# Idle TensorE matmuls around a Strassen-like feed-forward: two of 512 columns in place of eight groups

## The chip, the cores and the metric

The kernel runs on one core of a Trainium2 chip, in one launch. The metric is the device time of an execution in microseconds (us), the median of several runs. A profiled execution is one more execution, taken with the hardware profiler; its own time and its span (first to last instruction) are given beside the median. TensorE does matmuls, VectorE (DVE) and ScalarE (ACT) do elementwise work, GpSimd (POOL) and SyncE (SP) mostly issue DMAs.

## The reference

One encoder layer on 512 tokens of 1024 features, in float32, cut to its outline:

```python
n = rms_norm(h, mix_norm_g); proj = n @ w_in            # 1024 -> 512 + 4 * 1024
ya = s5_branch(...)                                     # state-space scan, both directions, + GLU
yb = sgu_branch(...)                                    # gated mixing within chunks of 128 tokens
h = h + (gate_a * (ya @ w_proj_a) + gate_b * (yb @ w_proj_b)) @ w_out
h = h + memory_cross_attention(rms_norm(h), memn, w_q, w_k, w_v, w_xo)
h = h + (silu(hn @ w_gate) * (hn @ w_up)) @ w_down      # hn = rms_norm(h); d_ff = 2816
return rms_norm(h, final_norm_g)
```

The change lies in the last product but one: the gate and up parts of the feed-forward.

## The kernel before

Every float32 operand of a large product is split into a part `hi` rounded to the type fp32r (ACT copies, line 85) and a rest `lo` (DVE subtracts, line 86), and each product is three matmuls on TensorE, hi x hi, hi x lo and lo x hi, summed in one PSUM bank (`mm3`, lines 347 to 352, and `product`, 1267 to 1278). The weights come from HBM in blocks of 512 KB. A plan written out by hand lists all blocks in the order of use; `next_w` (322 to 333) hands out the next one, issues loads some entries ahead and splits two entries ahead. `tick` (445) runs work that was put off by `later`. The recording layer then orders each engine's instructions by a simulated timeline, except those that `in_order` pins to the program's order.

In the stage before, attention's output product adds to the residual rows `h`. As each block of 128 rows is complete, it is normalised and turned by TensorE (`to_feat`, line 509: tiles `ptr`, four transposes each), and ACT and DVE write it as `fn`, features by tokens, split into `fn_hi` and `fn_lo` (lines 511 and 512), and whole as `full` (513). The last rows' turnings fall between the first matmuls of the feed-forward.

Gate and up have 2816 columns each. The last 256 columns are computed directly: `gate_part` (1458) for the gate, in two halves of the tokens, T0 and T1, and `feat` (1474) for up; these are the `pf` matmuls of line 350. The other 2560 columns are ten jobs (`UNITS`, line 313), gate and up in turn, 512 columns each. A job is a product of 2 x 2 blocks (token halves by feature halves K0 and K1, and by column halves) with seven block products in place of eight. Their operands are kept in `ops`: products 1, 2, 4 and 7 read parts of `fn`, products 5, 6 and 3 read sums of parts, kept in tiles `s`. Each of the seven is one call of `product`, 24 matmuls of 256 columns on banks `px`, `pv` or `pq`; "a block" below is such a call. The loop over the jobs (1531 to 1575) runs the products in the order 5, 6, the next job's 1, 7, the next job's 2, 4, 3. Product 1 of the first job (`unit_start`, 1465) and its product 2 (`unit_second`, 1467) stand between the gate's parts. In the first job K0's half for T1 is overwritten by a difference (line 1542), which product 7 reads from then on.

Between the blocks of the second and the third job (i = 1 and 2) the kernel runs idle work on TensorE: `between` (1522 to 1529) takes an idle bank and issues, by a string, transposes of the identity (`t`) or a matmul of 512 columns on `fn` (`p`), pinned in order. Nothing reads the results. The strings are "tt", then "p" or "pt", then "t" or "ttt", then "tttt" or "tt": eight groups, 15 transposes and 2 matmuls.

Behind the jobs the down product (lines 1634 to 1672) uses seven block products too, in matmuls of 512 columns on banks `dx`, `dv` and `dq` (line 350); two of its chunks are already run within the last job.

Idle tiles, the turnings and the up part's banks come in turn from one pool of three PSUM banks (`aux`, line 80).

Of the kernel before, what the change touches and what calls it, by code (L numbers as in the profile page):

```python
# [17 lines left out]
P = 128  # L18
# [34 lines left out]
def hybrid_layer_kernel(  # L53
# [8 lines left out]
    nc = tc.nc  # L62
# [14 lines left out]
    def bank(name):  # L77
        return pm.tile([P, 512], F32, tag="mm", name=name)

    def aux(name, shape=(P, 512)):  # L80
        return pa.tile(list(shape), F32, tag="aux", name=name)

    def split(dst_hi, dst_lo, src):

        hi = nc.scalar.copy(dst_hi, src)  # L85
        lo = nc.vector.tensor_tensor(dst_lo, src, dst_hi.bitcast(F32), ALU.subtract)  # L86
        if pinned[0]:
            in_order(hi)
            in_order(lo)
# [3 lines left out]
    in_order = tc.keep_in_program_order  # L93
# [228 lines left out]
    def next_w(*key):  # L322
        i = used_w[0]
        used_w[0] += 1
        assert len(plan[i][0]) == len(key) and plan[i][0][1:] == key[1:] and plan[i][0][0] is key[0]
        for j in range(i, min(i + FAR + 1, len(plan))):
            begin(j, i)
            if j - 1 >= len(tiles) and j - 1 <= i + SPLITS:
                split_w(j - 1)
        for j in range(len(tiles), min(i + SPLITS + 1, len(plan))):  # L330
            split_w(j)
        tile_, tiles[i] = tiles[i], None
        return tile_
# [45 lines left out]
    def feat_block(ps, x, act, nk, kpt, tsl, fresh=True):  # L379

        kb, hi, lo = x
        for j in range(2):
            cs = slice(j * P, (j + 1) * P)
            for k in range(kpt):
                kk = kb + k
                mm3(ps[j][:, tsl], (hi[:, k, cs], lo[:, k, cs]), (act[0][:, kk, tsl], act[1][:, kk, tsl]),
                    kk == 0 and fresh, kk == nk - 1, not fresh)
# [57 lines left out]
    def tick(us=5.2):  # L445

        side["now"] += us / 5.2
        run_due()
        side["credit"] = min(side["credit"] + us * side["rate"], us)
        while side["credit"] > 0.0 and side["gen"] is not None:  # L450
            try:
                used = next(side["gen"])
            except StopIteration:
                side["gen"] = None
                return
            if used is None:
                side["credit"] = 0.0
                return
            side["credit"] -= used
# [6 lines left out]
    ident = cp.tile([P, P], F32, name="ident")  # L466
# [58 lines left out]
    def token_slot(name, off=(0, 0)):  # L525

        return halves_at(sp.tile([P, 2 * KD * T + 128], F32R, tag="B", name=name), KD, T, off)
# [6 lines left out]
    idle = aux("idle", (P, P))  # L534
# [732 lines left out]
    def product(ps, u, q, start, ops):  # L1267

        hi, lo = next_w(u[0], u[1], q)
        for j in range(2):  # L1270
            cs = slice(j * P, (j + 1) * P)
            for k in range(4):
                a = (hi[:, k, cs], lo[:, k, cs])
                b = (ops[q][0][:, k, :], ops[q][1][:, k, :])
                for i, (x, y) in enumerate(((0, 0), (0, 1), (1, 0))):
                    nc.tensor.matmul(ps[:, j, :], a[x], b[y], start=start and j == k == i == 0,  # L1276
                                     stop=k == 3 and i == 2, skip_group_check=True)
        tick(2.7)

    def unit_bank(name):  # L1280
        return bank(name).rearrange("p (j t) -> p j t", j=2)
# [79 lines left out]
    fn_hi, fn_lo = token_slot("fn", APART)  # L1361
# [37 lines left out]
    def acts(unit, f):  # L1399

        if unit < 4:
            return (a_up, a_lo_)[f][:, 2 * unit:2 * unit + 2, :]
        if not rest:
            rest.append(fp.tile([P, KD, T], F32, tag="full", name="rest", bufs=1))
        return rest[0][:, 2 * f:2 * f + 2, :]
# [23 lines left out]
    def sum4():  # L1429
        V.tensor_tensor(a12, a12, a11, ALU.add)  # L1430
        make_op(3, 4, a12)

    fn_q = lambda ks, ts: (fn_hi[:, ks, ts], fn_lo[:, ks, ts])
    ops = {1: fn_q(K0, T0), 2: fn_q(K1, T0), 7: fn_q(K0, T1), 4: fn_q(K1, T1)}

    def unit_start(u):
        x, v = unit_bank("px"), unit_bank("pv")
        product(x, u, 1, True, ops)
        nc.scalar.copy(v, x)
        return x, v  # L1440

    def put(u, f, ts, src):
        dst = acts(u[1] // 512, f)[:, :, ts]
        if u[0] is w_gate:
            nc.scalar.activation(dst, src, AF.Silu)
        else:
            nc.vector.tensor_tensor(dst, dst, src, ALU.mult)

    def unit_second(u, v):
        product(v, u, 2, False, ops)  # L1450
        put(u, 0, T0, v)
# [6 lines left out]
    def gate_part(i, ts):  # L1458
        if ts is T0:
            ws.append((4 * i,) + next_w(w_gate, 4 * i, 4, FS, 256))  # L1460
        feat_block(ps, ws[i], fn, KD, 4, ts, ts is T0)
        tick(2.7)

    gate_part(0, T0)
    begun = unit_start(UNITS[0])
    gate_part(1, T0)
    unit_second(UNITS[0], begun[1])
    for i in range(2):
        gate_part(i, T1)
    for j in range(2):  # L1470
# [15 lines left out]
    def make_tokens(q, c):  # L1486

        if c % 2 or (q, c // 2) in made or (q, c) == (1, 0) and not last_job:
            return
        c //= 2  # L1490
        hi, lo = made[q, c] = sums_place((1, 2, 4)[len(made) % 3], 4, 256)
        f, ts = {1: (0, T0), 5: (0, T1), 6: (0, T1), 2: (1, T0), 7: (0, T0), 3: (1, T0), 4: (1, T1)}[q]
        for src, ks in token_pieces(f, ts, c):
            split(hi[:, ks], lo[:, ks], src)
        a, b_, c_, d_ = (token_pieces(f_, ts_, c) for ts_ in (T0, T1) for f_ in (0, 1))
        for (q11, _), (q12, _), (s21, _), (q22, _) in zip(a, b_, c_, d_):
            if q == 5:
                V.tensor_tensor(s21, s21, q11, ALU.subtract)
            elif q == 3:
                V.scalar_tensor_tensor(q11, s21, -1.0, q22, ALU.mult, ALU.subtract)  # L1500
            elif q == 2:
                V.tensor_tensor(q12, q12, s21, ALU.add)
# [14 lines left out]
    def down_product(ps, q, start, chunks=range(CHUNKS)):  # L1517
        for c in chunks:
            rows_product(ps, q, c, next_w(w_down, q, c), (0, 1), slice(0, 512), start and c == 0, c == CHUNKS - 1,
                         chunks[0] == c > 0)  # L1520

    def between(*what):

        rest_ = aux("idle")
        for w in what:
            if w == "t":
                in_order(nc.tensor.transpose(rest_[:, 0:P], ident, ident))
            else:
                in_order(nc.tensor.matmul(rest_, ops[1][0][:, 0, 0:P], fn_hi[:, 0, :], start=True, stop=True))

    for i, u in enumerate(UNITS):
        final = i == len(UNITS) - 1
        x, v = begun
        q = unit_bank("pq")
        if i in (1, 2):
            between(*"tt")
        product(q, u, 5, True, ops)
        if final:
            last_job.append(u)
            make_tokens(1, 0)  # L1540
        if i == 0:
            split(*fn_q(K0, T1), s3)
        if i in (1, 2):
            between(*"pt"[:i])
        product(x, u, 6, False, ops)
        u2 = stp[0].tile([P, 2, 256], F32, tag="u2", name="u2", bufs=2)
        u3 = np_.tile([P, 2, 256], F32, tag="ev", name="u3", bufs=2)
        nc.scalar.copy(u2, x)
        if not final:
            begun = unit_start(UNITS[i + 1])  # L1550
        else:
            dx = [bank(f"dx{t}") for t in range(2)]
            down_product(dx, 1, True, range(1))
        if i in (1, 2):
            between(*"tttt"[:i * 2 - 1])
        product(x, u, 7, False, ops)
        nc.scalar.copy(u3, x)
        if i == 0:
            sum4()
        if not final:  # L1560
            unit_second(UNITS[i + 1], begun[1])
        else:
            down_product(dx, 1, True, range(1, 2))
        V.tensor_tensor(u3, q, u3, ALU.subtract)
        put(u, 1, T1, u3)
        if i in (1, 2):
            between(*("tttt", "tt")[i - 1])
        product(x, u, 4, False, ops)
        put(u, 0, T1, x)
        if u[0] is w_up:  # L1570
            a_, b_ = (acts(u[1] // 512, f)[:, :, T1] for f in (0, 1))
            V.tensor_tensor(a_, a_, b_, ALU.subtract)
        product(q, u, 3, False, ops)
        V.tensor_tensor(u2, q, u2, ALU.subtract)
        put(u, 1, T0, u2)
# [131 lines left out]
```

## Time and profile before

| | |
|---|---|
| median of 3 runs | 908.49 us (908.34 to 910.14) |
| profiled execution, its own time | 908.83 us |
| its span | 907.0 us |
| TensorE busy | 895.5 us |
| DVE, ACT busy | 623.5, 475.6 us |
| HBM read, written | 146.08, 38.24 MB |
| start of the gate part for T1, start of w_down | at 588.02, 785.49 us of the span |

The profile gives an engine's busy time as the union of its instructions. Matmuls are pipelined, and their ends are modelled, so a matmul's mean duration says less than the distance of the starts: a stretch of TensorE's work divided by the number of matmuls in it is the pace. In the chain that ended last, each piece is a start, a length, the line that ran, and how many instructions were merged; where TensorE is the chain, the lengths add up to the clock on the wall. Windows give each engine's busy time in a stretch with the clock that the throttle granted to TensorE.

### The profile page before, as it was taken

To read this page: it belongs to the slowest core of one execution; us is meant where nothing else is said; L and a number is where in the kernel's file an instruction comes from. 1 tells how busy PE (TensorE), PEld (TensorE's weight loads), DVE (VectorE), ACT (ScalarE), POOL (GpSimd) and SP (SyncE) were. 2 spreads that over 40 slices of the span, in tenths; PEclk is the share of its full clock that TensorE was granted. 3 is DMA by queue.
4 is the path that set the end of the run, shared out by engine and by line. 5 is a ranking of instruction groups with operands and counts; after the bars stand their busy time and mean duration, and the time that the engine had idled before them with its cause. 6 is when DMAs were issued, how large, how long until landed. Compare 5 with 4: busy or idle time off the path is not lost.

```text
span 907.0 us, 14526 instructions
## 1 busy us (share of the span) xinstructions
PE 895.5 (99%) x5659; PEld 791.6 (87%) x5659; DVE 623.5 (69%) x1018; ACT 475.6 (52%) x696; POOL 104.3 (12%) x165
## 2 busy tenths in 40 slices
PE   9999999999999999999999999999999999999996
PEld 6878888888888887889999978999999999988885
DVE  5696662888753235858956836786778777799875
ACT  5543985144375244446655635655455455565664
POOL 1004320110025301011001001100011100000010
PEclk9999999999999999999999999999999999999999
DMA  7566574586546577863569416527678984246672
GB/s 238 172 161 178 125 179 138 164 201 156 141 135 153 130 198 225 279 190 119 173 221 278 138 51 186 154 58 185 163 198 222 221 198 116 70 139 198 199 234 101
DMA packets 111718, 153.80 MB, mean 170 GB/s; under 512 B 13521, under 2 KB 78561, under 8 KB 111586
## 3 DMA queue, kind: packets, MB, share of 16 engines
q1 hardware_dynamic: 92450, 127.22, 44.4%
q0 software_dynamic: 16608, 24.62, 16.7%
q10 hardware_dynamic: 2592, 1.05, 0.5%
q8 instruction: 44, 0.72, 0.3%
q14 instruction: 24, 0.20, 0.1%
HBM read 146.08 MB, written 38.24 MB: 203 GB/s over the span
## 4 chain that ended last, share of the span: by engine, by line
PE 92%; ACT 3%; DMA 2%; issue 1%; DVE 1%; POOL 0%; SPq 0%; POOLq 0%; DVEq 0%; ACTq 0%
PE pf L350 28%; PE pt L350 16%; PE px L1276 12%; PE dx L350 6%; PE pq L1276 6%; PE dq L350 3%; PE pv L1276 3%; PE qx L1276 2%; PE dv L350 2%; PE pk L789 2%; PE ptr L509 1%; PE psc L350 1%; PE qq L1276 1%; PE po L350 1%; DMA xt<-in_x_dram 1%
## 5 line engine op out<-in xcount | busy, mean ns | idle before, releaser
L86 DVE TENSOR_TENSOR wlo<-wraw,whi 128x1024 fp32r<-128x1024 f32 (+1 forms) x139 | 165.1, 1188 | 109.2 <-ACT whi L85 107.6
L85 ACT CAST whi<-wraw 128x1024 fp32r<-128x1024 f32 (+1 forms) x139 | 142.5, 1025 | 163.1 <-PE pf L350 70.5
L350 PE MATMUL pf<-xn,whi 128*128 128x512 f32 x448 | 140.0, 392 | 0.0
L350 PEld LDWEIGHTS pf<-xn,whi 128*128 128x128 f32 x448 | 83.5, 188 | 17.0 <-issue 0.2
L350 PE MATMUL pf<-xn,wlo 128*128 128x512 f32 x224 | 87.4, 390 | 0.0
L1276 PE MATMUL px<-fn,whi 128*128 128x256 f32 x480 | 84.4, 278 | 0.0
L1276 PEld LDWEIGHTS px<-fn,whi 128*128 128x128 f32 x480 | 72.8, 188 | 0.2
L85 ACT CAST whi<-b 128x1024 fp32r<-128x1024 f32 x40 | 42.2, 1054 | 54.5 <-PE px L1276 29.2
L86 DVE TENSOR_TENSOR wlo<-b,whi 128x1024 fp32r<-128x1024 f32 x40 | 48.9, 1223 | 31.4 <-ACT whi L85 31.4
L1276 PE MATMUL px<-fn,wlo 128*128 128x256 f32 x240 | 66.7, 278 | 0.0
L1276 PE MATMUL pq<-s,whi 128*128 128x256 f32 x320 | 55.7, 278 | 0.0
L350 PE MATMUL dx<-whi,s 128*128 128x512 f32 x170 | 53.6, 391 | 0.4 <-DVE h L1632 0.4
L86 DVE TENSOR_TENSOR wlo<-t,whi 128x1024 fp32r<-128x1024 f32 x30 | 36.7, 1224 | 19.9 <-ACT whi L85 19.9
L85 ACT CAST whi<-t 128x1024 fp32r<-128x1024 f32 x30 | 31.6, 1053 | 35.6 <-PE pv L1276 12.6
L350 PEld LDWEIGHTS pf<-xn,wlo 128*128 128x128 f32 x224 | 42.1, 188 | 8.7
L1276 PEld LDWEIGHTS pq<-s,whi 128*128 128x128 f32 x320 | 48.4, 188 | 0.0
L1276 PEld LDWEIGHTS px<-fn,wlo 128*128 128x128 f32 x240 | 45.2, 188 | 0.0
L1276 PE MATMUL pq<-s,wlo 128*128 128x256 f32 x160 | 44.4, 277 | 0.0
L350 PE MATMUL pt<-whi,xn 128*128 128x512 f32 x128 | 43.6, 412 | 0.1
L350 PEld LDWEIGHTS dx<-whi,s 128*128 128x128 f32 x170 | 31.8, 188 | 7.3 <-issue 0.8
L350 PE MATMUL dx<-wlo,s 128*128 128x512 f32 x85 | 33.1, 391 | 0.0
L1276 PEld LDWEIGHTS pq<-s,wlo 128*128 128x128 f32 x160 | 30.1, 188 | 0.0
(420 smaller groups left out, 2239.2 us busy)
## 6 DMA issues: line engine op xcount, KB each, us to landing
wraw<-in_w_in_dram SPq DMA_DIRECT2D x36, 512.0 KB, 4.3
dsum<-in_w_down_dram SPq DMA_DIRECT2D x20, 512.0 KB, 6.2
wraw<-dsum SPq DMA_DIRECT2D x20, 512.0 KB, 4.4
b<-in_w_gate_dram SPq DMA_DIRECT2D x15, 512.0 KB, 4.7
b<-in_w_up_dram SPq DMA_DIRECT2D x15, 512.0 KB, 4.5
wraw<-in_w_down_dram SPq DMA_DIRECT2D x15, 512.0 KB, 3.6
dsum<-in_w_down_dram POOLq DMA_DIRECT2D x10, 512.0 KB, 7.1
dsum<-dsum POOLq DMA_DIRECT2D x10, 512.0 KB, 6.6
```

Source lines behind the costliest of these rows:

```text
L85: hi = nc.scalar.copy(dst_hi, src)
L86: lo = nc.vector.tensor_tensor(dst_lo, src, dst_hi.bitcast(F32), ALU.subtract)
L350: m = nc.tensor.matmul(ps, a[x], b[y], start=start and i == 0, stop=stop and i == 2, skip_group_check=free)
L509: nc.tensor.transpose(ps[:, j, :], src[:, k * P:(k + 1) * P], ident)
L789: nc.tensor.matmul(ps[32 * j:32 * j + 32, q, :], bd[i][:, g].rearrange("p d c -> p (d c)"), lc(es[i], g), start=(i == 0), stop=False, tile ...
L1276: nc.tensor.matmul(ps[:, j, :], a[x], b[y], start=start and j == k == i == 0, stop=k == 3 and i == 2, skip_group_check=True)
```

## The change

A new `between`, without arguments, is defined ahead of the gate's parts. It issues one idle matmul of 512 columns, pinned in order, whose moving operand is chunk 4 of `fn_hi` (the first of K1, all tokens) where it was chunk 0. It is called once behind product 2 of the first job, ahead of the gate's part for T1, and once in the first job between products 5 and 6. The old `between` and its four calls in each of the second and third job are gone.

```diff
+    def between():
+
+        in_order(nc.tensor.matmul(aux("idle"), ops[1][0][:, 0, 0:P], fn_hi[:, 4, :], start=True, stop=True))
+
     gate_part(0, T0)
     begun = unit_start(UNITS[0])
     gate_part(1, T0)
     unit_second(UNITS[0], begun[1])
+    between()
     for i in range(2):
         gate_part(i, T1)
...
-    def between(*what):
-
-        rest_ = aux("idle")
-        for w in what:
-            if w == "t":
-                in_order(nc.tensor.transpose(rest_[:, 0:P], ident, ident))
-            else:
-                in_order(nc.tensor.matmul(rest_, ops[1][0][:, 0, 0:P], fn_hi[:, 0, :], start=True, stop=True))
-
     for i, u in enumerate(UNITS):
...
-        if i in (1, 2):
-            between(*"tt")
         product(q, u, 5, True, ops)
...
         if i == 0:
             split(*fn_q(K0, T1), s3)
-        if i in (1, 2):
-            between(*"pt"[:i])
+            between()
         product(x, u, 6, False, ops)
...
-        if i in (1, 2):
-            between(*"tttt"[:i * 2 - 1])
         product(x, u, 7, False, ops)
...
-        if i in (1, 2):
-            between(*("tttt", "tt")[i - 1])
         product(x, u, 4, False, ops)
```

The order of the other engines' instructions and of the DMAs in every queue is the same in both kernels; on TensorE the order differs by the idle instructions alone.

## The prediction

> **What bounds the kernel now.** I read the page first: who is busy, and at which clock.
>
> ```profile
> PE 895.5 (99%) x5659; PEld 791.6 (87%) x5659; DVE 623.5 (69%) x1018; ACT 475.6 (52%) x696; POOL 104.3 (12%) x165
> ...
> PEclk9999999999999999999999999999999999999999
> ```
>
> TensorE works through 99% of the span at the full granted clock; no other engine is near. The view of who waited for whom names no wait of TensorE from 574 to 785 us, where all edits lie. So the end moves by exactly what the stream of matmuls there gains or loses. Then the windows over that stretch: length, TensorE's busy time (instructions), its weight loads, DVE, ACT, POOL, clock, DMA.
>
> ```profile
> 588.02:604.98 16.96, 16.96 (x146) 16.96 (x145) 12.40 (x11) 9.23 (x10) 0.00 (x0) 1.00 0.18 28
> 604.98:624.77 19.79, 19.79 (x170) 19.79 (x169) 15.02 (x16) 9.97 (x12) 2.20 (x2) 1.00 0.71 190
> 624.77:663.09 38.32, 38.32 (x332) 38.21 (x330) 26.72 (x28) 18.15 (x22) 3.37 (x3) 1.00 0.68 164
> 663.09:785.49 122.40, 122.40 (x1083) 122.40 (x1081) 95.31 (x95) 64.99 (x78) 12.84 (x13) 1.00 0.71 169
> ```
>
> TensorE fills each row and the clock is 1.00 in each, yet the pace differs. That shows in the chain that ended last, in order of time (start, length, what; xN matmuls):
>
> ```profile
> 588.18 16.96 PE pf L350 x144
> 605.14 2.83 PE pq L1276 x24
> ...
> 624.93 0.22 PE idle L1527 x2
> 625.15 2.83 PE pq L1276 x24
> 627.98 0.23 PE idle L1529
> 628.21 5.45 PE px L1276 x48
> ...
> 639.25 0.44 PE idle L1527 x4
> 639.69 2.83 PE px L1276 x24
> ...
> 660.29 0.22 PE idle L1527 x2
> 660.51 2.74 PE px L1276 x24
> 663.25 5.44 PE pq L1276 x48
> ```
>
> 16.96 / 144 = 117.78 ns and 5.44 / 48 = 113.33 ns, for matmuls of one shape (256 columns) on the same operands. TensorE has **two gears** here. It stays in one until something odd passes: 117.78 from the last turning (584) to 627.8, 113.33 behind the 512-column idle matmul, slow again behind four idle transposes (639), and fast for good behind two (660): 1080 matmuls up to 785.49, 122.40 / 1080 = 113.33.
>
> **What selects the gear.** I took the starts of the matmuls in the trace to the nanosecond. All steady gaps are multiples of 6.667 ns: 17 (113.33), 34 (226.67, the fast 512-column matmul), and three gaps of the slow gear make 53 (353.33). So I divide each start by 6.667 ns and keep the remainder. In the fast gear it is the same for every start; in the slow one it runs through three places, averaged over 584.49 to 624.65: **2.0, 6.3, 3.7** and 2.0 again. The old 512-column matmul began at 627.820, remainder 6.7, so in the place 6.3. It lasted 230 ns, which is one slow step from there (117.3 by the trace) and 113.3 more; the next start (628.050) has 3.3, the next place of the cycle, and from there two gaps of 116 and 114 led to 113.3. My reading: an idle matmul in the slow gear moves the cycle by one place like any other, and gives the weight loads 113 ns in which to get ahead; entered at 6.3, that is enough to change gear.
>
> **The change part by part.**
>
> Removed: eight groups (15 transposes, two matmuls). From 588.02 to 663.09 are 75.07 us with 26 blocks of 24 matmuls, 624. Six blocks are in fast stretches (four from 628.05 to 639.09, one at 645.32, one at 660.26): 144 x 113.33 = 16.32; 480 x 117.78 = 56.53. The rest, 75.07 - 72.85 = 2.22 us, is what the groups cost, the delay of the matmul behind each included (first gaps of 200 to 204 ns behind transposes). Nothing covers it, as TensorE is the bound: -2.22.
>
> Added: two matmuls of 512 columns, one ahead of the gate's second token half (588.02 in before), one ahead of the first px block on s (607.81). Rows: 226.7 (fast 512-column matmuls), 230 and 235 (the two old ones). I take 0.23 each, as they enter from the slow gear like the first: +0.46, between 0.45 and 0.47.
>
> Waits: the first reads fn of all rows, whose last parts ACT writes here, and takes a bank whose last readers are ACT's copies.
>
> ```profile
> 583.77 1.27 ACT L85 CAST fn<-ptr 128x512 fp32r<-128x512 f32 x2 [0.15 <-PE ptr L509]
> 585.11 1.27 ACT L513 COPY full<-ptr 128x512 f32<-128x512 f32 x2
> ```
>
> Both are over by 586.38, 1.6 us ahead; the matmul behind it waited for the same casts. Without that cover the whole TensorE queue would stand for the delay. The second waits for the first alone, 20 us old, and reads the upper half of fn, which the first job doesn't rewrite. No other engine's order changes, and no DMA moves in any queue. The banks that the idle tiles shift go to the up product of 593.67 and to w_down's, read out long before.
>
> What is late next: the splits must follow a stream 4% faster from 588 or 608. The row from 663.09 shows ten-job work at that pace without a wait, with DVE at 78%; the earlier rows have DVE at 73 and 76%. Cost nothing; if a split slipped, by some tenths.
>
> Gear: the first matmul would enter at 588.022, remainder 2.0. By the reading it ends one place on, at 6.3, in a slow gear whose cycle has moved by one. 168 matmuls follow (56 full cycles), so the second enters at 6.3, the place from which the old one changed gear, and everything behind it is fast. Slow: 168 x 117.78 = 19.79; fast: 456 x 113.33 = 51.68. Against 480 in the slow gear now that is 312 x 4.44 ns = -1.39.
>
> Sum: 19.79 + 51.68 + 0.46 = 71.93 for 75.07, or -2.22 + 0.46 - 1.39 = **-3.15 us**. Behind 663.09 the gear is fast in both. The profiled execution took 908.83 (span 907.0 and 1.83 around it): 905.68. It lies 0.34 above the median of 908.49; from the median it is **905.4**.
>
> A rule speaks against all this. The trace's gaps are 113.33 or 117.78 for 256 columns, by history. The Trainium skill, page "TensorE: Matmul & The Clock Gate", section "Back-to-back issue gap", gives a warm gap by columns alone, N / 2.4 + 2.5 ns, so an estimate of 109.2 and 215.8 ns; by it no idle matmul could change its neighbours' pace. The trace agrees with neither figure, and shows two for one N.
>
> **The rivals.**
>
> *Fast from the first matmul on, and kept.* The weight loads get ahead at 588 already, and the second disturbs nothing. For it: 512 columns did change the gear at once at 627.82. Against: the other place of entry, and that a matmul entering the fast gear can upset it (the group at 648.14, one matmul and one transpose, turned fast into slow). 624 x 113.33 + 0.47 = 71.19: -3.88, so 904.6.
>
> *Never fast: slower than before.* In the slow gear 512-column matmuls that enter at the place 2.0 need not take the slow step. The first dx matmul of 791.17 entered there and took 227, and kept its place; and blocks of 256 columns behind such matmuls are slow:
>
> ```profile
> 788.51 2.83 PE px L1276 x24
> 791.34 2.72 PE dx L350 x12
> 794.06 2.83 PE px L1276 x24
> ```
>
> If the idle ones do likewise, both leave the cycle as it was. All 624 stay slow, 73.49 + 0.45 = 73.94 (-1.13), and with no transpose left to turn them, so do the 1080 behind 663.09: 1080 x 4.44 = +4.80. Together +3.67: 912.2. It decides at the gap behind 607.81: if that stays at 118, the loss runs to 785. Against it: dx reads other tiles at other addresses, and the one idle matmul seen alone did take the step.
>
> *Fast, then slow.* The first changes the gear, the second, entering the fast gear, changes it back, as at 648.14. 168 x 113.33 + 456 x 117.78 + 0.47 = 73.22 (-1.85), and +4.80: +2.95, so 911.4.
>
> *The idle work's own time alone.* The gears are set by something else in the same places, and the change doesn't do what it does by my reading: -2.22 + 0.46 = -1.76, 906.7. It is what the page's rule comes to. Against it: each change of gear from 620 to 785 stands right behind an idle group.
>
> **How the numbers follow.** Forecast 0.42; fast from the first 0.20; never fast 0.21; fast, then slow 0.13; own time alone 0.04. A measurement of this kernel tells some 0.2% (1.8 us) from no change: faster 0.62, same 0.04, slower 0.34. The likeliest case alone: 905.0 to 905.8 (the idle matmuls' bounds and the spread of runs). Cases of both signs hold the chance, and without the slowest 0.21 would be left out, so the range reaches from 904.4 to 912.3.
>
> **What would show it.** In the chain of the changed kernel: pf x144 still at 117.8 and the first idle matmul near 230 (227 speaks for never fast); the second near 230, and from there 113.3 up to the end of the jobs, the first dx near 782.3 instead of 785.5; no wait of TensorE at either idle matmul. Wrong would be: pf at 113.3 behind the first; px blocks of 2.83 us behind the second; or a wait on a split ahead of 625.

## The result and the profile after

The changed kernel takes 905.18 us (median of 7 runs, 904.29 to 907.09) where the kernel before, timed again with it, takes 909.82 (median of 7, 908.34 to 910.97): a ratio of 0.9954, 95% interval 0.9944 to 0.9964. The forecast was 905.4. The profiled execution took 906.38, with a span of 904.6.

The time is as forecast; the way to it is not. First the page of the changed kernel, the row of busy times:

```profile
PE 889.0 (98%) x5644; PEld 786.4 (87%) x5644; DVE 623.3 (69%) x1018; ACT 475.5 (53%) x696; POOL 103.5 (11%) x165
```

TensorE lost 6.5 us of busy time (895.5 to 889.0) and 15 instructions net (17 idle ones went, two came); the other engines moved by 0.8 us at most. Not all of the 6.5 is gain: 3.3 of it lie in the first 100 us, where the windows give 95.45 us busy for 98.73. There this execution waited longer for its first loads, and still reached the stretch of the edits only 0.19 us later. The windows over the stretch of the edits, from the first idle matmul to the first `dx` (length, TensorE busy, weight loads, DVE, ACT, POOL, clock, DMA):

```profile
588.21:604.79 16.58, 16.58 (x148) 16.53 (x147) 12.30 (x11) 9.29 (x10) 0.00 (x0) 1.00 0.18 29
604.79:624.00 19.21, 19.21 (x171) 19.17 (x170) 14.76 (x16) 9.96 (x12) 2.20 (x2) 1.00 0.70 193
624.00:659.60 35.60, 35.60 (x317) 35.60 (x316) 26.86 (x28) 18.27 (x22) 2.88 (x3) 1.00 0.71 180
659.60:781.83 122.23, 122.23 (x1081) 122.23 (x1080) 95.41 (x95) 65.11 (x78) 13.24 (x13) 1.00 0.70 169
```

The clock is 1.00 in all four, as before, and TensorE fills each row, so no split is late. Their sum is 193.62 us; the same stretch of the kernel before is 785.49 - 588.02 = 197.47. That is -3.85 us, not the forecast's -3.15. The chain that ended last tells why (start, length, what):

```profile
588.38 0.23 PE idle L1466
588.61 16.34 PE pf L350 x144
604.95 2.72 PE pq L1276 x24
607.67 0.23 PE idle L1466
607.90 8.17 PE px L1276 x72
616.07 2.72 PE pv L1276 x24
618.79 2.72 PE px L1276 x24
621.51 5.44 PE pq L1276 x48
626.95 8.16 PE px L1276 x72
```

`pf` x144 lasts 16.34 us, 113.5 ns each with the transition, where it lasted 16.96: the first idle matmul already turned the pace, and it stays at 113.33 past the second one (px x72 in 8.17, 113.5 each) up to 781.83. This is the rival "fast from the first matmul on, and kept", whose sum was -3.88.

Outside the stretch the profiled execution gave part of it back: from the first `dx` to the end are 122.77 us where they were 121.51. The section on the reasons comes back to it.

### The profile page after: what moved, and what is told of

The parts are those of the page before. It is cut to its first block, busy times and chain, and to the rows that moved or that the text cites. A ratio compares the mean times of both kernels' runs of the same rounds, so it can differ in the third digit from the quotient of the medians.

```text
span 904.6 us, 14497 instructions
## 1 busy us (share of the span) xinstructions
PE 889.0 (98%) x5644; PEld 786.4 (87%) x5644; DVE 623.3 (69%) x1018; ACT 475.5 (53%) x696; POOL 103.5 (11%) x165
## 4 chain that ended last, share of the span: by engine, by line
PE 89%; ACT 4%; DMA 2%; DVE 1%; issue 1%; SPq 1%; POOL 1%; POOLq 0%; DVEq 0%; ACTq 0%
PE pf L350 28%; PE pt L350 16%; PE px L1276 12%; PE pq L1276 6%; PE dx L350 5%; PE dq L350 3%; PE pv L1276 3%; PE qx L1276 2%; PE dv L350 2%; PE pk L789 2%; PE psc L350 1%; PE qq L1276 1%; PE ptr L509 1%; DMA slab<-in_s_log_step_dram 1%; PE po L350 1%
## 5 line engine op out<-in xcount | busy, mean ns | idle before, releaser
L350 PEld LDWEIGHTS pt<-whi,xn 128*128 128x128 f32 x128 | 24.0, 190 | 8.2 <-ACT whi L85 2.0
```

The costliest lines, as they stand in the source:

```text
L350: m = nc.tensor.matmul(ps, a[x], b[y], start=start and i == 0, stop=stop and i == 2, skip_group_check=free)
```

## The experiments

All start from the changed kernel. Since whole times of one kernel spread over 0.8 to 4.2 us where it ran four times or more, the table also has a length from the trace, in which all the edits lie but the one in the key product, and no wait that varies: from the start of the last turning (the last `ptr` matmul) to the first `dx`. 1704 matmuls of 256 columns lie between the gate part for T1 and the first `dx`; at 117.78 in place of 113.33 ns they cost 7.57 us more.

| kernel | last turning to first dx, us | median, us (runs) | ratio to before, 95% interval |
|---|---|---|---|
| before | 201.34 | 909.82 (7) | |
| changed | 197.50 | 905.18 (7) | 0.9954 (0.9944 to 0.9964) |
| e_first | 197.25 | 905.11 (5) | 0.9956 (0.9944 to 0.9969) |
| e_second | 198.00 | 906.21 (4) | 0.9964 (0.9950 to 0.9978) |
| e_none | 204.57 | 912.07 (7) | 1.0032 (1.0021 to 1.0044) |
| e_256 | 204.69 | 913.28 (4) | 1.0042 (1.0028 to 1.0056) |
| e_384 | 204.75 | 912.69 (4) | 1.0033 (1.0005 to 1.0061) |
| e_place | 197.35 | 905.94 (6) | 0.9964 (0.9944 to 0.9984) |
| e_wst | 197.24 | 904.99 (6) | 0.9958 (0.9943 to 0.9974) |
| e_wmov | 204.80 | 912.73 (3) | 1.0041 (1.0007 to 1.0075) |
| e_walign | 197.25 | 904.96 (2) | 0.9948 (0.9930 to 0.9966) |
| e_fnoff | 204.80 | 912.79 (3) | 1.0037 (1.0022 to 1.0052) |
| e_wk | 197.25 | 904.30 (5) | 0.9941 (0.9927 to 0.9954) |
| e_wk64 | 197.25 | 905.01 (5) | 0.9954 (0.9940 to 0.9967) |

The kernel before was timed again with each group of kernels, at 908.8 to 910.2; the ratios are to those runs.

### One of the two, or neither

e_first leaves out the second call:

```diff
             split(*fn_q(K0, T1), s3)
-            between()
```

> The changed kernel without its second idle matmul: only the one ahead of the gate part for T1 is left. Theory A (512 columns in a row let the weight loads get ahead, wherever the matmul enters; nothing afterwards turns the pace back): pf x144 again 16.34 us, 113.33 ns for all 256-column matmuls up to the first dx, the stretch from the gate part for T1 to the first dx 193.37 us (193.62 less the 0.235 of the second matmul and some 0.01 of gaps behind it), time 0.25 us below the changed kernel, 904.9 from its median of 905.2. Theory B (my prediction's reading: a matmul that enters at the place 2.0 only moves the cycle by one place, and the second one did the turning): pf x144 at 117.78, 16.96 us, and all 1704 matmuls slow: 1704 x 4.44 = +7.57, less 0.25, 912.5. Theory C (the pace is set by place, not by idle matmuls): 904.9 as A, but then the kernel with none gives the same.

Measured: as A says, 197.25 us against 197.50. The chain of e_first:

```profile
589.78 0.23 PE idle L1466
590.01 16.34 PE pf L350 x144
```

The second idle matmul costs 0.25 us and brings nothing. The medians (905.11 and 905.18) can't show so little; the trace does.

e_second leaves out the first call:

```diff
     unit_second(UNITS[0], begun[1])
-    between()
     for i in range(2):
```

> The changed kernel without its first idle matmul: only the one between products 5 and 6 of the first job is left. It enters 168 matmuls later, which are 56 full cycles, so at the same place 2.0 as the first did. Theory A (512 columns turn the pace from any place): pf x144 16.96 us, 168 matmuls at 117.78 (+0.75 us), then the idle one some 236 ns, gaps of 123 and 116 behind it, and 113.33 to the end; +0.75 - 0.25 = +0.50 against the changed kernel, 905.7. Theory B (the place 2.0 alone doesn't turn it; something in the gate's part for T1 did): 117.78 to the end, +7.3, 912.5. Theory C (place in the program): fast from 588 without it, 904.9.

Measured: 198.00, which is 0.50 more than the changed kernel, as A says (the median of 906.21 lies above the 905.7 expected, within the spread of its four runs, 905.36 to 907.48). The chain of e_second:

```profile
588.71 16.96 PE pf L350 x144
605.67 2.83 PE pq L1276 x24
608.50 0.23 PE idle L1466
608.74 8.18 PE px L1276 x72
616.91 2.72 PE pv L1276 x24
```

168 matmuls at 117.8 ns ahead of it, 113.6 in the first 72 behind (the transition among them) and 113.3 from then on: the same turn in another place of the program, from the same place 2.0 of the cycle.

e_none leaves out both calls.

> The changed kernel without either idle matmul: no idle work between the turnings and the down product. Theory A and theory B alike: nothing turns the pace, so pf x144 16.96 us and all 1704 matmuls of 256 columns up to the first dx at 117.78 where the changed kernel has 113.33: 7.57 less 0.48 for the two idle ones and their next gaps, +7.1, 912.3; the stretch from the gate part to the first dx 200.7 us; that is 3.2 to 3.8 us slower than the kernel before. Theory C (the idle matmuls cost their own time alone): -0.48, 904.7, 4 us faster than the kernel before.

Measured: 204.57 and 912.07. The chain:

```profile
587.39 16.96 PE pf L350 x144
604.35 2.83 PE pq L1276 x24
607.18 8.48 PE px L1276 x72
615.66 2.83 PE pv L1276 x24
```

Without any idle work the pace is 117.8 up to the first `dx`, and the kernel is slower than with the eight old groups. One idle matmul of 0.235 us is worth 204.57 - 197.25 = 7.32 us, that is 1704 x 4.44 less its own time. Theory C, that idle work costs its own time alone, is off by 7 us. The rule that the prediction weighed (the Trainium skill, page "TensorE: Matmul & The Clock Gate", section "Back-to-back issue gap") gives a warm gap by the columns alone, but for an isolated matmul; of a stream of weight loads and matmuls the section says that both set the spacing. The traces bear out that the columns alone don't set it here: e_none and e_first run the same matmuls at 117.78 and at 113.33.

### What the idle matmul must be

e_256 and e_384 change the number of columns (with the first call alone):

```diff
-        in_order(nc.tensor.matmul(aux("idle"), ops[1][0][:, 0, 0:P], fn_hi[:, 4, :], start=True, stop=True))
+        in_order(nc.tensor.matmul(aux("idle")[:, 0:256], ops[1][0][:, 0, 0:P], fn_hi[:, 4, 0:256], start=True, stop=True))
```

> The first idle matmul alone, with 256 columns in place of 512 (the moving operand is the T0 half of the same chunk). Theory A in its narrow form (what turns the pace is the time that a matmul of more than 256 columns gives the weight loads): 256 columns give none, the pace stays at 117.78 up to the first dx, 1704 x 4.44 = +7.57, less 0.24 for the second, less 0.12 for the shorter first: +7.2, 912.4. Theory D (any matmul out of the pattern turns it: another bank, another operand address, one more step): fast from 588 on, 0.36 below the changed kernel, 904.8. Theory B: slow, with the cycle moved by one place, 912.4.

> The first idle matmul alone, with 384 columns in place of 512. Theory A4 (anything longer than the pattern's 256 columns gives enough time): some 170 to 180 ns (384/512 of the 226.7 ns of a fast one, and up to 10 more), then 113.33 up to the first dx, 905.1. Theory A5 (the full 113 ns of 256 more columns are needed): 117.78 throughout, 7.4 more, 912.5.

Measured: neither turns the pace. 204.69 and 204.75 are e_none plus 0.12 and plus 0.18, the idle matmuls' own time. In e_384's chain:

```profile
588.16 0.17 PE idle L1466
588.34 16.96 PE pf L350 x144
```

So theory D (any matmul out of the pattern) and A4 (anything longer than 256) fall; between 384 and 512 columns the border wasn't looked for.

e_place puts an idle matmul of 256 columns right ahead of the one of 512, so that the latter enters one place further on, at 6.3.

> The first idle matmul alone, with another idle one of 256 columns right ahead of it: the 256 one takes one slow step, so the 512 one enters at the place 6.3 in place of 2.0, as the old one at 627.82 of the kernel before did. Theory A (512 columns turn the pace from any place): idle matmul 230 ns, gaps of 116 and 114 behind it, 113.33 up to the first dx; 905.1 + 0.12 = 905.2. Theory B2 (the place 2.0 is what lets it turn here): 117.78 throughout, 912.6.

Measured: turned, 197.35 (e_first plus 0.10). The idle one took 231 ns with a gap of 116 behind it, as the old one at 627.82 in before (230 and 116); from the place 2.0 it is 236, 123, 116 and 116 (changed kernel, e_first, e_second). Of the two places tried, neither keeps the turn from coming; the place sets a few ns of the transition.

The next two exchange one operand each. The weights `whi` of the product just before are kept in reach (`product.w = hi`):

```diff
+        in_order(nc.tensor.matmul(aux("idle"), ops[1][0][:, 0, 0:P], product.w[:, 0:2, :], start=True, stop=True))   # e_wmov
+        in_order(nc.tensor.matmul(aux("idle"), product.w[:, 0, 0:P], fn_hi[:, 4, :], start=True, stop=True))         # e_wst
```

> The first idle matmul alone, with 512 columns of the weights of the product before it as its moving operand, in place of fn (the stationary operand stays fn). Theory A1 (512 columns turn the pace whatever is read): idle matmul 236 ns, then gaps of 123 and 116 and 113.33 up to the first dx; 905.1 as with fn. Theory A2 (the moving operand decides: the 512-column matmuls of the down product, which move weights, leave the blocks behind them at 117.8): idle matmul 227 ns with the place kept, 117.78 for all 1704 matmuls, 905.1 + 7.4 = 912.5.

> The first idle matmul alone, with 128 columns of the weights of the product before it as its stationary operand, in place of fn (the moving operand stays fn, 512 columns). Theory A1 (any 512 columns) and theory A2 (the moving operand decides): turned at once, 113.33 up to the first dx, 905.1. Theory A3 (the stationary operand decides, by where its tile lies): 117.78 throughout, 912.5.

Measured: the moving operand decides. e_wst is as e_first (197.24). e_wmov is e_none plus 0.23 (204.80), though its idle matmul took 230 ns and not the 227 expected. The chain of e_wst, and then that of e_wmov:

```profile
587.83 0.23 PE idle L1466
588.06 16.33 PE pf L350 x144
```


```profile
588.32 0.23 PE idle L1466
588.55 16.96 PE pf L350 x144
```

The weight tiles and `fn` differ in two ways: in what they are, and in where they begin. In each partition `fn_hi` begins at a multiple of 128 elements (of 4 bytes) and `fn_lo` 64 past one, and the weight tiles begin 80 past one. These addresses are those of the program built from the kernel; no view of the profile has them. e_walign moves the weights from column 48 on, which is a multiple of 128 again; e_fnoff moves `fn` from 80 on:

```diff
+        ... product.w.rearrange("p k n -> p (k n)")[:, 48:560] ...                 # e_walign
+        ... fn_hi[:, 4:6, :].rearrange("p k n -> p (k n)")[:, 80:592] ...          # e_fnoff
```

> The first idle matmul alone, moving the same weight tile as in e_wmov, but from column 48 of the tile on (columns 48 to 559). The weight tiles begin 80 elements past a multiple of 128 elements in each partition, fn on one; 48 columns on, the moving operand begins on one too. Theory A2a (the address of the moving operand decides): now it turns the pace as fn does, idle matmul 234 to 236 ns, 113.33 up to the first dx, 905.1. Theory A2b (the tile decides, whatever the address: another buffer, another way of being written): 117.78 throughout as in e_wmov, 912.7.

> The first idle matmul alone, moving fn, but 512 columns that begin 80 elements past the multiple of 128 elements where chunk 4 begins, as the weight tiles do. Theory A2a (the address of the moving operand decides): as e_wmov, idle matmul 230 ns and 117.78 throughout, 912.7. Theory A2b (the tile decides): turned, 234 to 236 ns and 113.33 up to the first dx, 905.1.

Measured: the address decides, in both directions. The chain of e_walign, and then that of e_fnoff:

```profile
588.13 0.23 PE idle L1466
588.37 16.34 PE pf L350 x144
```

```profile
587.92 0.23 PE idle L1466
588.15 16.96 PE pf L350 x144
```

The same tile, 48 columns on, turns the pace, and the tile that turned it no longer does 80 columns on; 7.55 us lie between them (204.80 - 197.25).

### A version that beats both

e_wk keeps the first idle matmul, and adds one some 155 us earlier, in the key product of the memory attention, where the profile of before has the same pattern: turnings, then matmuls at 117.8 ns. The edit, with its condition written out as an `if`:

```diff
                 feat_block(ps, ws.pop(), act, nk, kpt, slice(0, n))
                 tick(5.2 * n / T)
+                if w is w_k and c0 == 512 and kb == 0:
+                    in_order(nc.tensor.matmul(aux("idle"), act[0][:, 0, 0:P], act[0][:, 0:2, :], start=True, stop=True))
```

> A version meant to beat both kernels: the first idle matmul as in the changed kernel, not the second, and one more of 512 columns in the key product of the memory attention, some 155 us earlier, where 92 matmuls of 256 columns run at 117.78 ns behind the last turning of that stage and 96 of 512 columns after them at 233.33 ns. It moves the memory tokens, which lie at the same address class as fn, and stands 72 matmuls ahead of the 512-column ones. Theory A (it turns the pace there too, and the 512-column ones inherit it): 72 x 4.44 = 0.32, 96 x 6.67 = 0.64, less 0.24 for itself: 0.72 below the kernel with the first one alone, 905.11 - 0.72 = 904.4. Rival (the 512-column ones of that product are slow by their own operands, weights at the other address class): 0.32 - 0.24 = 0.08 below, 905.0. Rival (the turning only works behind the feed-forward's turnings): 0.24 above, 905.35.

Measured: 904.30 (903.95 to 904.76). The chain of e_first in that stage, and then that of e_wk:

```profile
432.38 10.96 PE pf L350 x93
443.34 22.40 PE pt L350 x96
```

```profile
430.67 2.48 PE pf L350 x21
433.14 0.23 PE idle L371
433.37 8.16 PE pf L350 x72
441.54 21.97 PE pt L350 x96
```

It turned the pace there too: 72 matmuls at 113.4 ns from start to start. With itself counted that saves 10.96 - 10.87 = 0.09 us, as expected. The 96 matmuls of 512 columns behind (`pt`, which move weights) took 21.97 in place of 22.40: 228.9 ns each, between the 233.3 they had and the 226.7 I expected, in gaps of 226, 229 and 232 in turn. So neither reading of them was right: what runs ahead matters for them, but they did not come to the fastest pace. In all 0.52 us in place of 0.72. The medians differ by 0.8 us (904.30 and 905.11), but the two kernels were timed in different groups, and their runs spread over 0.8 and 1.8 us.

e_wk64 is e_wk with `fn_lo[:, 0, :]` as the moving operand of the feed-forward's idle matmul.

> The version of e_wk once more, with one thing changed: the idle matmul ahead of the gate part for T1 moves the lo rest of fn, whose rows begin 64 elements past a multiple of 128 (the normal blocks move operands of both classes, 0 and 64). Theory A2a in its narrow form (a multiple of 128 elements is needed): 117.78 up to the first dx, 1704 x 4.44 = 7.57 slower than e_wk, 911.9; from the last turning to the first dx 204.8 us. Theory A2a in its wide form (a multiple of 64 is enough): turned, last turning to first dx 197.25 us as in e_wk, 904.3. The key product's idle matmul is as in e_wk: 433 to 463 us again 0.5 us shorter than without it.

Measured: 197.25, so a multiple of 64 elements is enough, and `pf` x144 takes 16.34 us behind it. The stage of the key product repeated itself (`pt` x96 in 21.97 again). The median is 905.01 (903.22 to 905.52), so over both versions the whole time is 903.2 to 905.5: below the kernel before for certain, and below the changed kernel by the 0.25 + 0.52 us that the traces show, which these medians alone would not settle.

## Why the prediction was right, and where it was wrong

**Removed groups, -2.22, and the two added matmuls, +0.46: right.** An idle matmul costs its own length: e_none, e_256, e_384 and e_wmov differ in this alone, and stand at 204.57, +0.12, +0.18 and +0.23. The two of the changed kernel took 236 and 235 ns, 0.47 in all. e_none shows the other term without them: it lacks the eight groups and is slow throughout, so 144 + 1080 matmuls cost 4.44 ns more than in before, 5.44 us; less 2.22 that makes +3.22, and 204.57 - 201.34 is 3.23. With the gear's term as measured, the two terms add up to the stretch: -2.22 + 0.47 - 480 x 4.44 ns (2.13) makes -3.88; it was -3.85.

**Waits: right.** The view of who waited for whom shows none on TensorE from 574 to 782 us, though the stream is 4% faster from 588 on.

**Gear, -1.39: this step failed.** The prediction said that the first matmul, entering at the place 2.0, only moves the cycle by one place, that 168 matmuls stay in the slow gear, and that the second, entering at 6.3, does the turning. It rested on a single event in the trace of before, and took for its cause what was only its place. (The pair of stretches in which it first read the two gears, `pf` and `pq`, moves `fn` and `s`, so not the same operands, as it says; e_none and e_first are a pair that has them the same.) e_first and e_second, which enter at 2.0, and e_place, which enters at 6.3, show that 512 columns turn the gear from both; the third place wasn't tried. The term measures -2.13 in place of -1.39, and the second matmul was not needed.

**"It gives the weight loads 113 ns in which to get ahead": not shown.** That 512 columns are needed and 384 are not would fit it. But it says nothing of addresses, and those decide. In the records a weight load begins some 3 ns after the matmul ahead of it in both gears, so a lead can't be seen there. One trace of the gears is in the loads' lengths (min/median/max in ns, 590 to 780 us; e_wmov, then e_walign):

```profile
L1276 PEld LDWEIGHTS px<-fn,whi x430: 187/190/192, 610.9 to 779.9; 128*128 128x128 f32 x144
```

```profile
L1276 PEld LDWEIGHTS px<-fn,whi x432: 187/188/188, 609.9 to 772.8; 128*128 128x128 f32 x144
```

2 ns of median is less than the 4.44 ns of the pace, and which is cause and which effect these lines don't tell.

**The rival "never fast": its mechanism exists, its case was not this one.** It argued from the `dx` matmuls of 512 columns, which leave the blocks behind them at 117.8, and named the other addresses of `dx` as the point against. That was the right point: `dx` moves weights that begin at 80, and an idle matmul that does so (e_wmov, e_fnoff) ends in that rival's time, 912.7 and 912.8 for 912.2. Had the change moved a weight tile, the forecast would have been wrong by 7 us and in sign.

**The rival "fast, then slow":** the second one entered the fast gear, took 235 ns, and 122 and then 115 behind it, and left the gear as it was. In before the group at 648.14 was a matmul and a transpose, and the pace behind it was slow. The matmul alone doesn't turn the gear back, which leaves the transpose or the two together; that was not tried by itself, and a transpose alone in the fast gear, at 633.50, left it fast (gaps of 113 to 114 ns from the sixth on). From the chain of before:

```profile
633.66 0.11 PE idle L1527
633.77 2.76 PE px L1276 x24
...
645.35 0.22 PE idle L1527 x2
645.56 2.74 PE pq L1276 x24
648.30 0.23 PE idle L1529
648.54 0.11 PE idle L1527
648.64 5.66 PE px L1276 x48
```

The lines show more: two idle transposes in the slow gear turned it to fast at 645, as those at 660 did, while the two at 624.77 did not. So a long idle matmul isn't the only thing that turns the pace, and what decides among the transposes is open.

**The end.** The profiled execution of the changed kernel has 1.26 us more from the first `dx` on, so its own time fell by 2.45 and not by 3.85 (a later start of the stretch adds 0.19). It waits for a split, behind a DMA that the chain shows, in the changed kernel and then in e_256:

```profile
874.20 6.99 DMA wraw<-dsum
881.28 1.06 ACT whi L85
882.37 1.24 DVE wlo L86
```

```profile
882.56 6.84 DMA wraw<-dsum
```

e_256 is at 117.8 throughout and waits as long: a start-to-start gap of 1.22 us on TensorE there and 1.26 in the changed kernel, where its pace is 0.23. The same gap is 1.15 in e_walign, 0.90 in e_second, 0.72 in e_none, 0.68 in e_fnoff, 0.60 in e_wmov, 0.58 in e_first, 0.48 in e_wk, and doesn't appear above 0.40 in before, e_wst, e_384, e_place and e_wk64. So it is not the price of the faster stream. It varies by execution in either gear; what makes this DMA late in some is open. With the start of the stretch, which lies between 583.4 and 585.7 us at the last turning over these traces, it makes most of the spread of the whole times.

That the forecast of 905.4 came within 0.2 us of the median is luck in part. Two errors of opposite sign stand in it: 0.7 us of gear not counted, and a tail that in the profiled execution took more than that. From the median of 908.49 that the prediction started from, -3.15 is 905.34 and -3.85 would be 904.6; the runs' median is 905.18, and which part of those 0.5 us is the tail's and which the spread of seven runs, they don't tell. And the start itself moved: the runs of before that were timed with the changed kernel have a median of 909.82, from which -3.15 is 906.67 and -3.85 is 905.97. The medians' own difference is 4.64 us, more than either. The stretch in the trace shows what the change is worth, and the medians agree with it to about a microsecond.

## What to carry to other kernels

Divide a stretch of back-to-back matmuls by their number and compare equal shapes: two paces for one shape at a granted clock of 1.00 are a stretch that one idle matmul may mend, and 4.44 ns each are worth it from some 55 matmuls on (0.235 / 0.00444 = 53). Of those tried, the ones that did it have 512 columns whose moving operand begins at a multiple of 64 elements in the partition. The earlier in the slow stretch it stands, the more it is worth (here soon behind the last turning); one is enough, and a second costs its 0.25 us. Where a trace shows one event, find out by one run each what of it counts (its place, its size, its operands) before building on it: here the place was taken for the cause, and the address was it.

## What the hardware showed that I had not expected

- The address at which a moving operand begins decides whether a 512-column matmul turns the pace of the 256-column ones behind it: 0 and 64 elements past a multiple of 128 do (e_walign, e_wk64), 80 past it doesn't (e_wmov, e_fnoff), whichever tile it is; the stationary operand's address doesn't matter (e_wst). Other offsets weren't tried, and why it is so stays open.
- The pace then lasts: 1701 matmuls in a row at 113.33 ns in e_first, 1704 at 117.78 in e_256, with neither drifting into the other.
- Matmuls of 512 columns have a third pace: 228.9 ns (e_wk, `pt`), beside 226.7 and 233.3 for the same shape.
